# Relative bias, low-rank weights and projection steps rearranged around RWKV in a hybrid RWKV-7 / FoX / DSA layer

## Chip, cores and metric

The kernel runs on one core of a Trainium2 chip, in one launch. The metric is device time in microseconds (us), median of several runs; lower is better.

## The reference

One layer over 1024 prompt rows and 64 sample rows (the latter with 512 cached rows): `u = RMSNorm(h)`, one projection `z = u @ W_in` for all branches, three mixers on slices of `z`, and `h + W_out . concat(gated mixers)`, normed again. The parts that the change touches:

```python
def rwkv7_mixer(z, shift_prev, wkv0, mu, w0, w_b, a0, a_b, ...):
    zm = z + (prev - z) * mu
    r, k, v, w_in, a_in = jnp.split(zm, ...)
    decay = jnp.exp(-jnp.exp(-softplus(-(w0 + jnp.tanh(w_in) @ w_b)) - 0.5))
    a = jax.nn.sigmoid(a0 + a_in @ a_b)
    ...
def dsa_attention(q, k, v, q_idx, k_idx, w_idx, t5_table, q_pos, k_pos):
    ...
    bias = t5_table[t5_bucket(pos_sel - q_pos)]
    s = jnp.where(valid, s + bias, -jnp.inf)
```

A is RWKV-7, whose decay and rate come from two low-rank products (`w_b`, `a_b`, 64 x 512 each); B is FoX, softmax attention with a forget gate; C is DSA, sparse attention over the keys that an indexer picks, with a T5 relative bias.

## The kernel before, in words

The program goes through these stages: load and norm; the indexer of C (`indexer`); RWKV in 17 units of four 64-row chunks each; FoX; DSA and output. The projection runs beside all of them as a fill. A column group of 128 is projected in steps: each step of `proj` is one `yield` and three matmuls (L154), for the high part of `u` and the weights and the two cross terms. `pump(n)` adds `n` to a credit (at most 8) and deals one step for each whole credit, so a stage's rate sets how many steps lie between its own pieces. Rate 70 (capped) holds in the indexer, `R_A` = 7 in the preparation of the first unit (prep0), `R_A / 10` = 0.7 for each piece that `braid` deals in RWKV's units. `tied` writes edges that hold a dealt step behind the piece before it; within these edges a scheduler orders every engine's instructions.

Weights for a column group come through `load_w`: a load into one of two raw buffers (L130, SyncE), a cast to the high part on ScalarE (L137), and the low part and a bf16 copy on POOL (L140, L142). ScalarE also evicts projection banks (L802), with VectorE's L803 behind it.

The relative bias (`relative_bias`, L1242) is a 32x8 table times a one-hot, 8 x 384 (L1254), copied to `t5v`, and written to the DRAM buffer `d_t5`, 128 times the same rows (L1258): one transfer from 8 partitions. DSA reads `d_t5` at the other end of the kernel.

`rwkv_pools` (L1260) loads the low-rank weights twice over (`wabr`, four transfers, L1275), casts them on ScalarE (`wabh`, L1276) and subtracts on POOL (`wabl`, L1278). `low_rank` multiplies with both (L1293, L1294). A unit's inversion (`chunk_invert`) has five levels: a product (L1478) that VectorE masks (Y, L1509), then products with Y (L1471) that VectorE subtracts (U, L1518). The state chain has products at L1559, L1564 and L1572 with VectorE between them.

The lines of the fill's rate, in `pump` and in the loop over the units:

```python
self.credit = min(self.credit + n, 8)
while self.credit >= 1 and self.fill:
    ...
s.weave(("prep0", s.prepare(units[0], x[0])), 10, R_A)
s.braid(work, R_T if u > n else R_END if len(work) < 3 and u else R_A / 10, ...)
```

Of the kernel before, what the change touches and what calls it, by code (L numbers as in the profile page):

```python
# [12 lines left out]
F32 = mybir.dt.float32  # L13
F32R = mybir.dt.float32r
# [4 lines left out]
OP = mybir.AluOpType  # L19
# [5 lines left out]
P = 128  # L25
# [60 lines left out]
class K:  # L86
# [103 lines left out]
    def pump(self, n):  # L190

        self.credit = min(self.credit + n, 8)
        while self.credit >= 1 and self.fill:
            self.mark(self.fill[0][0])
            if self.tied(self.fill[0][1], (PE,)):
                self.credit -= 1
            else:
                self.filled.add(self.fill.popleft()[0])
# [66 lines left out]
        self.now = None  # L265

    now = None


    def setup(self):  # L270
# [127 lines left out]
    def indexer(self):  # L398
# [6 lines left out]
        with ExitStack() as c2:  # L405
            ip, ip2 = self.ip, self.ip2
            pm = self.pool("idx_ps", bufs=3, space=PSUM, ctx=c2)
            KI = ip.tile([P, NKEY], F32R, name="KI")
            KIL = ip.tile([P, NKEY], F32R, name="KIL")
            QI = [ip.tile([P, 832], F32R, name=f"QI{h}") for h in range(4)]  # L410
            mT = ip.tile([P, NT], F32, name="mT")
            mrow = ip.tile([P, 9, 76], F32, name="mrow")
            wI = ip.tile([P, 9, 4], F32, name="wI")
            wm = self.get_w((COL["c_ki"], 68), (COL["b_f"], 8))
            wq = [self.get_w((COL["c_qi"] + 128 * j, 128)) for j in range(2)]

            def both(ps, t0, n):
                c = slice(t0, t0 + n)
                for r in (slice(0, 64), slice(64, 128)):
                    nc.scalar.copy(KI[r, c], ps[0:64, :n])  # L420
                    nc.vector.tensor_tensor(KIL[r, c], ps[0:64, :n], KI[0:64, c], op=OP.subtract)

            def keys(t0, n):
                ps = yield from self.proj(wm, t0, n)
                nc.scalar.copy(mT[:76, t0:t0 + n], ps[:76, :n])
                both(ps, t0, n)

            def queries(j, t0, n):
                ps = yield from self.proj(wq[j], t0, n)
                c0 = t0 - 256  # L430
                a, b = QI[2 * j], QI[2 * j + 1]
                nc.scalar.copy(a[0:64, c0:c0 + n], ps[0:64, :n])
                nc.scalar.copy(b[64:128, c0:c0 + n], ps[64:128, :n])
                nc.vector.tensor_tensor(a[64:128, c0:c0 + n], ps[0:64, :n], a[0:64, c0:c0 + n], op=OP.subtract)
                nc.vector.tensor_tensor(b[0:64, c0:c0 + n], ps[64:128, :n], b[64:128, c0:c0 + n], op=OP.subtract)


            yield from keys(0, 384)
            for j in range(2):
                yield from queries(j, 256, 384)  # L440
            yield from keys(384, 384)

            ps = self.tp()
            for a in range(4):
                nc.tensor.transpose(ps[:64, a * P:(a + 1) * P], self.kc[:, a, :], self.ident)
            both(ps, 1088, 512)
            yield from keys(768, 320)
            for j in range(2):
                yield from queries(j, 640, 448)
            for i in range(9):  # L450
                r = P if i < 8 else 64
                ps = self.tp()
                nc.tensor.transpose(ps[:r, :76], mT[:76, i * P:i * P + r], self.ident[:76, :76])
                nc.scalar.copy(mrow[:r, i, :], ps[:r, :76])
            nc.vector.memset(wI[64:128, 8, :], 0.0)
            nc.vector.tensor_scalar(wI[:, 0:8, :], mrow[:, 0:8, 64:68], 0.5, None, op0=OP.mult)
            nc.vector.tensor_scalar(wI[:64, 8, :], mrow[:64, 8, 64:68], 0.5, None, op0=OP.mult)
            self.fill.extend((f"a{j}", self.park_a(j)) for j in range(2))
            self.pump(8)
            for i in list(range(2, 8)) + ["s"]:  # L460

                if i == 3:
                    gates = self.forget(ip, mrow)
                    next(gates)
                    bias = self.relative_bias(c2)
                    next(bias)
                if i == 4:
                    nc.sync.dma_start(out=O["p_c_kidx"][0, 0].rearrange("(a p) d -> p a d", p=P), in_=mrow[:, 0:8, 0:64])
                    nc.sync.dma_start(out=O["s_c_kidx"][0, 0], in_=mrow[:64, 8, 0:64])
                if i == 5:  # L470
                    next(bias)
                if i == 7:
                    next(gates, None)
                if i == "s":
                    next(bias, None)
                r = P if i != "s" else 64
                q0 = i * P - 256 if i != "s" else 768
                k0, kn = (0, (i + 1) * P) if i != "s" else (1024, 576)
                wi = 8 if i == "s" else i
                for s0 in range(0, kn, 512):  # L480
                    n = min(512, kn - s0)
                    for h in range(4):
                        ps = pm.tile([P, 512], F32, tag="s", name="ps_idx")
                        nc.tensor.matmul(ps[:r, :n], QI[h][:, q0:q0 + r], KI[:, k0 + s0:k0 + s0 + n], start=True, stop=False)
                        nc.tensor.matmul(ps[:r, :n], QI[h][:, q0:q0 + r], KIL[:, k0 + s0:k0 + s0 + n], start=False, stop=True)
                        rl = ip2.tile([P, 512], F32, tag="rl", name="rl")
                        nc.scalar.activation(rl[:r, :n], ps[:r, :n], AF.Relu, scale=0.125)
                        dst = self.score[i][:r, s0:s0 + n]
                        if h == 0:
                            nc.vector.tensor_scalar(dst, rl[:r, :n], wI[:r, wi, 0:1], None, op0=OP.mult)  # L490
                        else:
                            nc.vector.scalar_tensor_tensor(dst, rl[:r, :n], wI[:r, wi, h:h + 1], dst, op0=OP.mult, op1=OP.add)
                        if h % 2:
                            yield
                if i != "s":
                    nc.vector.memset(self.score[i][0:64, kn - 64:kn], NEG)
# [745 lines left out]
    def relative_bias(self, ctx):  # L1242

        nc = self.nc
        self.d_t5 = self.dram.tile([P, 8, 384], F32, tag="d_t5", name="d_t5")
        p = self.pool("t5", ctx=ctx, right=True)
        pp = self.pool("t5p", space=PSUM, ctx=ctx, right=True)
# [7 lines left out]
        vv = p.tile([8, 384], F32, name="t5v")  # L1255
        nc.vector.tensor_copy(vv, ps[:8, :384])
        yield
        nc.sync.dma_start(out=self.d_t5.rearrange("q h r -> h q r"), in_=vv.rearrange("h (o r) -> h o r", o=1).broadcast_to([8, P, 384]))  # L1258


    def rwkv_pools(self, c2):

# [2 lines left out]
        one = self.pool("rw1", ctx=c2, right=True)  # L1265
        self.gen = self.pool("gen", space=PSUM, ctx=c2)
        self.gring = lambda tag, bufs: (lambda dt=F32: self.gen.tile([P, 512], dt, tag=tag, name="ps_" + tag, bufs=bufs))

        self.wabh = one.tile([P, 2, 512], F32R, name="wabh")
        self.wabl = one.tile([P, 2, 512], F32R, name="wabl")  # L1270
        nc.gpsimd.memset(self.wabl.bitcast(F32), 0.0)
        raw = self.z("wabr")[:, 0:1024].rearrange("p (x c) -> p x c", x=2)
        for x, nm in enumerate(("a_w_b", "a_a_b")):
            for r in (slice(0, 64), slice(64, 128)):
                nc.sync.dma_start(out=raw[r, x], in_=I[nm][0])  # L1275
        nc.scalar.copy(self.wabh, raw)  # L1276
        for x, r in enumerate((slice(0, 64), slice(64, 128))):
            nc.gpsimd.tensor_tensor(self.wabl[r, x], raw[r, x], self.wabh[r, x], op=OP.subtract)  # L1278
        self.one, self.state = one, None

        self.ND = [one.tile([P, 2, 4, P], F16, name=f"ND{i}") for i in range(2)]
# [474 lines left out]
def program(ctx, tc, I, O):  # L1756
    s = K(ctx, tc, I, O)
# [23 lines left out]
    s.setup()  # L1781
    cx.close()
    with ExitStack() as c2:
        s.zs = s.pool("zs", bufs=1, ctx=c2, right=True)
        s.scp = s.pool("scp", ctx=c2, right=True)
        s.tkp = s.pool("tkp", ctx=c2, right=True)
# [15 lines left out]
        topk = s.topk()  # L1802
        n = len(units)
        x = [dict(ND=s.ND[u % 2]) for u in range(n)]
        s.weave(("prep0", s.prepare(units[0], x[0])), 10, R_A)
        for u in range(n + 2):
            work = []
# [11 lines left out]
            if u < n:  # L1819
                work.append(("topk", topk, N_TOPK, (DVE, ACT)))  # L1820
            work = [w[:3] for w in work if w[0] != "topk"]
            s.free = u >= FE
            s.braid(work, R_T if u > n else R_END if len(work) < 3 and u else R_A / 10, ("topk", topk, N_TOPK, (DVE, ACT), work[-1][0] if SIDE < 0 else work[SIDE][0]) if u < n else None)
        for _ in topk:
            pass
        s.need("b0")
        for _ in range(PX):
            s.pump(8)
# [85 lines left out]
```

## Time and profile before

| what | value |
|---|---|
| median of 3 runs | 1330.21 us (1328.97 to 1335.14) |
| profiled execution, its own time | 1331.56 us |
| its span | 1329.8 us |
| TensorE (PE) busy | 1258.4 us, 95% |
| VectorE (DVE) busy | 847.5 us, 64% |
| ScalarE (ACT) busy | 780.2 us, 59% |
| GpSimd (POOL) busy | 669.7 us, 50% |
| DMA | 168.78 MB, mean 127 GB/s |
| mean granted TensorE clock | 0.979 |

The busy times are sums over the span of one profiled execution; the engines run beside each other. The span is what lies between the first and the last instruction, and the execution's own time has 1.8 us more around it. The granted clock is the share of TensorE's full speed that the chip let through.

### The profile page before, as it was taken

What the parts mean: (1) busy time and instruction counts of PE and PEld (TensorE: products, weight loads), DVE (VectorE), ACT (ScalarE), POOL (GpSimd) and SP (SyncE); (2) the same over time, 40 slices, a digit from 0 to 9 for tenths busy, and PEclk for the clock granted to TensorE, in tenths of its full rate; (3) what the DMA queues carried; (4) which work ended last, traced back from release to release, by engine and by line L of the source; (5) the groups of instructions that cost most, each with busy time, mean ns of one, the idle gap of its engine ahead of it and who ended that gap; (6) DMA issues with size and microseconds to landing.
All of it is one profiled execution on the core that took longest, in us unless ns stands there. A gap on an engine that the chain in (4) does not pass through costs nothing.

```text
span 1329.8 us, 29357 instructions
## 1 busy us (share of the span) xinstructions
PE 1258.4 (95%) x10544; PEld 964.2 (73%) x10563; DVE 847.5 (64%) x2487; ACT 780.2 (59%) x1762; POOL 669.7 (50%) x973
## 2 busy tenths in 40 slices
PE   7969999999999999988999998999999989999997
PEld 5747676777777777766777677888988856777764
DVE  7338437887877777899754316556666479766642
ACT  7335427777777887644353346576665578655532
POOL 6223445445445456556464365566667567544311
PEclk9979999999999999988999998999999989999999
DMA  7352422222223324433232378867755576543323
GB/s 224 50 105 71 128 83 66 87 70 89 68 70 104 102 80 140 123 101 110 94 104 89 126 216 246 217 201 209 182 198 146 146 212 186 142 116 106 97 76 95
DMA packets 172460, 168.78 MB, mean 127 GB/s; under 512 B 38513, under 2 KB 147097, under 8 KB 172314
## 3 DMA queue, kind: packets, MB, share of 16 engines
q1 hardware_dynamic: 172314, 166.89, 43.9%
q8 instruction: 84, 1.38, 0.4%
q14 instruction: 62, 0.51, 0.1%
HBM read 104.61 MB, written 62.24 MB: 125 GB/s over the span
## 4 chain that ended last, share of the span: by engine, by line
PE 73%; DVE 11%; DMA 6%; ACT 3%; issue 3%; POOL 2%; SPq 1%; DVEq 0%; POOLq 0%; ACTq 0%
PE pproj L154 32%; PE pproj L1697 7%; PE ps_pv L993 5%; PE ps_atp L107 5%; PE ps_tp L1697 4%; PE ps_ga L1412 3%; DMA wraw<-in_w_in_dram 2%; PE ps_sc L962 2%; PE ps_sc L963 2%; PE ps_gb L1471 2%; PE ps_tp L107 1%; PE ps_gb L1478 1%; PE ps_gc L1581 1%; ACT junka L601 1%; PE ps_gc L1583 1%
## 5 line engine op out<-in xcount | busy, mean ns | idle before, releaser
L154 PE MATMUL pproj<-uH,wh 128*128 128x384 f32 (+4 forms) x1088 | 494.6, 455 | 0.0
L154 PE MATMUL pproj<-uH,wl 128*128 128x384 f32 (+4 forms) x1088 | 363.4, 334 | 0.0
L154 PE MATMUL pproj<-uL,wb 128*128 128x384 bf16 (+4 forms) x1088 | 359.4, 330 | 2.2 <-DVE shift L806 2.0
L154 PEld LDWEIGHTS pproj<-uH,wh 128*128 128x128 f32 (+1 forms) x1088 | 217.9, 200 | 3.9 <-issue 0.7
L154 PEld LDWEIGHTS pproj<-uH,wl 128*128 128x128 f32 (+1 forms) x1088 | 208.1, 191 | 2.2 <-issue 0.2
L154 PEld LDWEIGHTS <-wb 128*128 128x128 bf16 (+1 forms) x1088 | 106.6, 98 | 118.6 <-issue 81.5
L601 ACT ACTIVATE junka<-score,tk_tau 128x1024 f16<-128x1024 f32 (+4 forms) x160 | 149.4, 934 | 38.9 <-DVE junk L595 24.1
L914 POOL TENSOR_SCALAR S<-S,mx 128x128 f32<-128x128 f32 (+8 forms) x136 | 103.8, 766 | 83.7 <-DVE mx L913 60.4
L931 ACT CAST hl<-ps_atp 128x512 fp32r<-128x512 f32 (+3 forms) x184 | 93.4, 514 | 77.7 <-PE ps_atp L107 68.2
L140 POOL TENSOR_TENSOR wl<-wraw,wh 128x256 fp32r<-128x256 f32 (+1 forms) x184 | 137.1, 775 | 3.3 <-ACT wh L137 2.7
L932 DVE TENSOR_TENSOR hl<-ps_atp,hl 128x512 fp32r<-128x512 f32 (+3 forms) x184 | 109.7, 600 | 44.6 <-ACT hl L931 42.8
L142 POOL TENSOR_SCALAR wb<-wraw 128x512 bf16<-128x512 f32 (+1 forms) x92 | 60.3, 671 | 142.1 <-issue 60.7
L909 ACT ACTIVATE S<-S,mx 128x128 f32<-128x128 f32 (+8 forms) x136 | 105.8, 778 | 38.2 <-DVE mx L905 34.8
L993 PE MATMUL ps_pv<-hl,VS 128*128 128x256 f32 (+3 forms) x640 | 113.7, 290 | 7.7 <-ACT hl L931 3.2
L993 PEld LDWEIGHTS ps_pv<-hl,VS 128*128 128x128 f32 (+1 forms) x640 | 90.4, 176 | 20.8 <-DVE hl L932 5.0
L107 PE MATMUL ps_atp<-ident,S 128*128 128x128 f32 x616 | 103.6, 280 | 1.1 <-POOL S L914 0.8
L1159 POOL TENSOR_TENSOR cb<-nm,T 128x256 f32<-128x256 bf16 (+2 forms) x80 | 57.4, 724 | 52.7 <-DVE mx L905 51.1
L107 PEld LDWEIGHTS ps_atp<-ident,S 128*128 128x128 f32 x616 | 76.4, 144 | 7.7 <-issue 1.7
L137 ACT CAST wh<-wraw 128x1024 fp32r<-128x1024 f32 (+1 forms) x46 | 47.7, 1038 | 47.0 <-PE pproj L154 27.0
L1697 PE MATMUL pproj<-oh,gh 128*128 128x512 f32 x144 | 67.4, 490 | 0.6 <-ACT pproj L1745 0.3
L803 DVE SCALAR_TENSOR_TENSOR zm<-pproj,omm,zs 128x384 f32<-128x384 f32 (+2 forms) x52 | 25.8, 496 | 43.3 <-ACT zs L802 42.9
L1697 PE MATMUL pproj<-ol,gb 128*128 128x512 bf16 (+1 forms) x134 | 48.8, 386 | 1.4 <-DVE ol L1677 0.9
(383 smaller groups left out, 2849.6 us busy)
## 6 DMA issues: line engine op xcount, KB each, us to landing
wraw<-in_w_in_dram SPq DMA_DIRECT2D x45, 512.0 KB
oraw<-in_w_out_dram SPq DMA_DIRECT2D x12, 512.0 KB
out_dram<-rows SPq DMA_DIRECT2D x10, 512.0 KB
x<-in_x_prompt_dram SPq DMA_DIRECT2D x8, 512.0 KB
wt<-a_wa SPq DMA_DIRECT2D x16, 256.0 KB
b_v<-vs SPq DMA_DIRECT2D x8, 512.0 KB
VS<-b_v SPq DMA_DIRECT2D x8, 512.0 KB
d_y<-y SPq DMA_DIRECT2D x64, 64.0 KB
```

What stands on the lines that cost most here:

```text
L107: self.nc.tensor.transpose(out, x, self.ident[:n, :n])
L140: nc.gpsimd.tensor_tensor(l[:, k:k + 2, :n], raw[:, k:k + 2, :n], h[:, k:k + 2, :n], op=OP.subtract)
L142: nc.gpsimd.tensor_scalar(b[:, k:k + 4, :n], raw[:, k:k + 4, :n], 1.0, 0.0, op0=OP.mult, op1=OP.add)
L154: self.nc.tensor.matmul(ps[:n, :nt], a[:, k, :n], b[:, k, t0:t0 + nt], start=(k == 0 and i == 0), stop=(k == KD - 1 and i == 2))
L601: nc.scalar.activation(junk[:, :sc.shape[1]], sc, AF.Sign, bias=tf[:, j:j + 1], accum_out=cnt[:, j:j + 1])
L909: nc.scalar.activation(S[:, :kn], S[:, :kn], AF.Exp, bias=mx[:, nm - 1:nm], scale=-1.0, accum_out=mx[:, 6:7])
L914: nc.gpsimd.tensor_scalar(S[:, :kn], S[:, :kn], mx[:, 7:8], 0.5, op0=OP.mult, op1=OP.mult)
L931: nc.scalar.copy(ph[:kr, a:b], ps[:kr, a:b])
L932: nc.vector.tensor_tensor(pl[:kr, a:b], ps[:kr, a:b], ph[:kr, a:b], op=OP.subtract)
L993: nc.tensor.matmul(pv[0:m, q0:256], VS[:, kb, 0:m], hl[:, x, o:o + w], start=kb == 0 and x == 0, stop=at[-1][0] == last and n == 3)
L1159: nc.gpsimd.tensor_tensor(o, x, y, op=OP.add)
L1697: nc.tensor.matmul(ps[hf][:n, :], parts[m // 4][q][:, m % 4, :n], self.wo[m][q // 2][:, hf * 512:hf * 512 + 512], start=m == 0 and q == 0, ...
```

## The change

It has three parts. The table's product goes to DRAM as a row of 12 KB (`d_row`) and is copied from there to `d_t5` in eight transfers of 16 rows, which the program text places one at a time at the start of RWKV's units 1 to 8. The low-rank weights are loaded, cast and subtracted in the indexer, in a pool of their own (`lr`), with the raw copy in the score buffer of the indexer's last query block. And `pump` gets a `burst`: with 2, from prep0 to the end of RWKV's loop, it deals only when two steps are due.

```diff
@@ pump
         self.credit = min(self.credit + n, 8)
+        if self.credit < self.burst:
+            return
         while self.credit >= 1 and self.fill:
@@ indexer
-                    bias = self.relative_bias(c2)
-                    next(bias)
+                    self.bias = self.relative_bias(c2)
+                    next(self.bias)
+                    self.load_low_rank()
                 if i == 5:
-                    next(bias)
+                    next(self.bias)
+                    self.split_low_rank()
                 if i == "s":
-                    next(bias, None)
+                    next(self.bias)
@@ relative_bias
+        row = self.dram.tile([8, 384], F32, tag="d_row", name="d_row")
         yield
-        nc.sync.dma_start(out=self.d_t5.rearrange("q h r -> h q r"), in_=vv.rearrange("h (o r) -> h o r", o=1).broadcast_to([8, P, 384]))
+        nc.sync.dma_start(out=row[:, :], in_=vv)
+        yield
+        for q in range(0, P, 16):
+            nc.sync.dma_start(out=self.d_t5[q:q + 16], in_=row.rearrange("(o h) r -> o h r", o=1).broadcast_to([16, 8, 384]))
+            yield
+    def load_low_rank(self):
+        nc, p = self.nc, self.lr
+        self.wabh = p.tile([P, 2, 512], F32R, name="wabh")
+        self.wabl = p.tile([P, 2, 512], F32R, name="wabl")
+        nc.gpsimd.memset(self.wabl.bitcast(F32), 0.0)
+        self.wabr = self.score[7].rearrange("p (x c) -> p x c", x=2)
+        for x, nm in enumerate(("a_w_b", "a_a_b")):
+            for r in (slice(0, 64), slice(64, 128)):
+                nc.sync.dma_start(out=self.wabr[r, x], in_=self.I[nm][0])
+    def split_low_rank(self):
+        nc = self.nc
+        nc.scalar.copy(self.wabh, self.wabr)
+        for x, r in enumerate((slice(0, 64), slice(64, 128))):
+            nc.gpsimd.tensor_tensor(self.wabl[r, x], self.wabr[r, x], self.wabh[r, x], op=OP.subtract)
@@ rwkv_pools
-        self.wabh = one.tile([P, 2, 512], F32R, name="wabh")
-        self.wabl = one.tile([P, 2, 512], F32R, name="wabl")
-        nc.gpsimd.memset(self.wabl.bitcast(F32), 0.0)
-        raw = self.z("wabr")[:, 0:1024].rearrange("p (x c) -> p x c", x=2)
-        for x, nm in enumerate(("a_w_b", "a_a_b")):
-            for r in (slice(0, 64), slice(64, 128)):
-                nc.sync.dma_start(out=raw[r, x], in_=I[nm][0])
-        nc.scalar.copy(self.wabh, raw)
-        for x, r in enumerate((slice(0, 64), slice(64, 128))):
-            nc.gpsimd.tensor_tensor(self.wabl[r, x], raw[r, x], self.wabh[r, x], op=OP.subtract)
@@ program
+        s.lr = s.pool("lr", ctx=c2, right=True)
+        s.burst = 2
         s.weave(("prep0", s.prepare(units[0], x[0])), 10, R_A)
+            if u:
+                next(s.bias, None)
             s.free = u >= FE
+        s.burst = 1
         s.need("b0")
```

What stands on the engines is set by the scheduler. On SyncE, in the indexer, before (t5tab and t5oh are the table and the one-hot, d_t the bias in DRAM, wraw a raw weight buffer, mrow the indexer's keys):

```order
L1250 DMA t5tab<-in_t_table_dram 32x8
L1251 DMA t5oh<-in_onehot_dram 32x384
L1258 DMA d_t_822<-t5v 8x128x384
L130 DMA wraw<-in_w_in_dram 128x8x128 x2
L468 DMA out_dram<-mrow 128x8x64
```

and in the changed kernel, where score_416 is the score buffer that holds the raw low-rank weights:

```order
L1257 DMA t5tab<-in_t_table_dram 32x8
L1258 DMA t5oh<-in_onehot_dram 32x384
L1281 DMA score_416<-in_a_w_b_dram 64x512 x2
L1281 DMA score_416<-in_a_a_b_dram 64x512 x2
L1265 DMA d_row<-t5v 8x384
L1268 DMA d_t_826<-d_row 16x3072 x8
L130 DMA wraw<-in_w_in_dram 128x8x128 x2
L473 DMA out_dram<-mrow 128x8x64
```

All eight copies stand together, ahead of the two weight loads, and not among RWKV's units; the low-rank loads have come up ahead of them.

On POOL, before, where the indexer ends and prep0 begins (ND are two buffers of the inversion, lw the log decay):

```order
L140 TENSOR_TENSOR wl<-wraw,wh 128x256 x4
L1271 MEMSET wabl 128x1024
L1283 MEMSET ND_1695 128x1024
L1283 MEMSET ND_1696 128x1024
L1325 MEMSET lw 128x4
L1278 TENSOR_TENSOR wabl<-wabr,wabh 64x512 x2
L1337 TENSOR_SCALAR lw<-lw 128x4x64
```

and in the changed kernel the same work well before that, in the middle of the indexer:

```order
L140 TENSOR_TENSOR wl<-wraw,wh 128x256 x4
L1277 MEMSET wabl 128x1024
L1287 TENSOR_TENSOR wabl<-score_416,wabh 64x512 x2
L142 TENSOR_SCALAR wb<-wraw 128x512 x2
L140 TENSOR_TENSOR wl<-wraw,wh 128x256 x4
```

The memset and the two subtractions have moved past seven groups of weights, to the gap ahead of the one whose wb follows.

On TensorE, in the first unit's inversion, before (the last product of one kind L1478 of a level, then what lies ahead of the products L1471 that need VectorE's Y):

```order
L1478 LDWEIGHTS ND_1695
L1478 MATMUL ps_gb<-T_2152,ND_1695 128x64
L1363 MATMUL ps_ga<-ident,arn 64x128 x4
L154 LDWEIGHTS wb
L154 MATMUL pproj<-uL,wb 128x384
L154 MATMUL pproj<-uH,wh 128x384
L154 MATMUL pproj<-uH,wl 128x384
L1471 LDWEIGHTS U_2163
L1471 MATMUL ps_gb<-Y_2170,U_2163 64x64
```

and in the changed kernel, where L1495 and L1488 are these lines:

```order
L1495 MATMUL ps_gb<-T_2152,ND_1698 128x64
L1495 LDWEIGHTS ND_1698
L1495 MATMUL ps_gb<-T_2152,ND_1698 128x64
L1488 LDWEIGHTS U_2163
L1488 MATMUL ps_gb<-Y_2173,U_2163 64x64
```

The projection step and the transposes (L1363) between the two have gone elsewhere. Over RWKV, runs of projection matmuls fall from 272 to 238 (runs of one step from 69 to 18).

## Rows read from the trace of the kernel before

**Rows 1.** The page's first part: busy us (share of the span) and instructions of each engine.

```profile
PE 1258.4 (95%) x10544; PEld 964.2 (73%) x10563; DVE 847.5 (64%) x2487; ACT 780.2 (59%) x1762; POOL 669.7 (50%) x973
```

**Rows 2.** The chain of waits from 40 to 175: start us, us, what.

```profile
57.80 26.16 DMA wraw<-in_w_in_dram
...
87.98 4.44 PE pproj L154 x13
...
158.80 4.26 DMA wabr<-in_a_a_b_dram
```

**Rows 3.** TensorE's timeline, 70 to 98: start, us, line, operation, [idle before <- releaser].

```profile
85.65 0.34 PE L453 MATMUL ps_tp<-ident,mT 76*64 76x76 f32 x1 [9.54 <-ACT mrow L454]
87.98 0.50 PE L154 MATMUL pproj<-uL,wb 128*128 128x384 bf16 x1 [2.00 <-DVE shift L806]
```

**Rows 4.** Windows: us, busy PE PEld DVE ACT POOL, granted clock, DMA share, GB/s.

```profile
70.00:75.00 5.00, 5.00 (x34) 3.75 (x33) 0.00 (x0) 0.00 (x0) 0.00 (x0) 1.00 0.44 49
...
175.00:180.00 5.00, 5.00 (x34) 3.37 (x32) 2.95 (x7) 0.58 (x1) 1.23 (x3) 1.00 0.88 270
...
87.98:92.42 4.44, 4.43 (x14) 3.21 (x15) 3.92 (x13) 3.73 (x8) 1.00 (x3) 0.50 0.48 122
165.70:171.30 5.60, 5.59 (x22) 4.49 (x22) 1.29 (x3) 2.74 (x6) 4.03 (x6) 0.50 0.07 21
```

**Rows 5.** TensorE's timeline from 332.8 to 334.3, in RWKV.

```profile
332.99 0.34 PE L154 MATMUL pproj<-uH,wl 128*128 128x384 f32 x1
333.16 0.34 PE L154 MATMUL pproj<-uL,wb 128*128 128x384 bf16 x1
...
333.51 0.34 PE L154 MATMUL pproj<-uH,wl 128*128 128x384 f32 x1
333.78 0.71 PE L1412 MATMUL ps_ga<-QR,BK 64*128 64x128 f32 x4
```

**Rows 6.** SyncE's queue (SPq), 38 to 100: start and length of an issue.

```profile
49.62 0.29 SPq L1258 DMA_DIRECT2D d_t<-t5v  x1
57.80 17.71 SPq L130 DMA_DIRECT2D wraw<-in_w_in_dram  x2
```

**Rows 7.** DMA issues: the write of the relative bias, KB each.

```profile
d_t<-t5v SPq DMA_DIRECT2D x1, 1536.0 KB
```

**Rows 8.** ScalarE's timeline, 66 to 90.

```profile
84.06 1.04 ACT L137 CAST wh<-wraw 128x1024 fp32r<-128x1024 f32 x1 [15.09 <-DMA wraw<-in_w_in_dram]
```

**Rows 9.** TensorE's timeline, 160 to 167, at the start of prep0.

```profile
164.32 0.38 PE L1293 MATMUL ps_ga<-wt,wabh 128*128 128x256 f32 x1 [2.12 <-ACT wabh L1276]
165.71 0.58 PE L1294 MATMUL ps_ga<-wt,wabl 128*128 128x256 f32 x1 [1.01 <-POOL wabl L1278]
```

**Rows 10.** ScalarE's and POOL's timelines, 155 to 170.

```profile
163.22 1.04 ACT L1276 CAST wabh<-wabr 128x1024 fp32r<-128x1024 f32 x1 [2.17 <-DMA wabr<-in_a_a_b_dram]
...
164.40 2.60 POOL L1278 TENSOR_TENSOR wabl<-wabr,wabh 64x512 fp32r<-64x512 f32 x2 [6.05 <-ACT wabh L1276]
```

**Rows 11.** Windows of RWKV: its bulk, and a stretch near its end.

```profile
200.00:560.00 360.00, 349.02 (x4145) 264.37 (x4143) 280.18 (x905) 281.31 (x646) 186.07 (x292) 1.00 0.30 92
...
600.00:625.00 25.00, 21.80 (x210) 15.97 (x210) 23.43 (x57) 12.08 (x33) 16.34 (x20) 0.87 0.26 71
```

**Rows 12.** ScalarE's and POOL's timelines in the indexer.

```profile
47.16 0.42 ACT L425 COPY mT<-pproj 76x320 f32<-76x320 f32 x1 [1.56 <-PE pproj L154]
...
53.64 1.20 POOL L142 TENSOR_SCALAR wb<-wraw 128x512 bf16<-128x512 f32 x2 [21.27 <-PE pproj L154]
```

**Rows 13.** Timeline of all engines, 247.6 to 249.6, in RWKV.

```profile
247.89 0.29 PE L1478 MATMUL ps_gb<-T,ND 128*128 128x64 f16 x4
...
248.22 0.42 DVE L1509 TENSOR_TENSOR Y<-ps_gb,con 128x256 f16<-128x256 f32 x1 [0.28 <-PE ps_gb L1478]
...
248.70 0.31 PE L1471 MATMUL ps_gb<-U,Y 64*64 64x64 f16 x8 [0.25 <-DVE Y L1509]
```

**Rows 14.** A window of the last stage.

```profile
1070.00:1080.00 10.00, 8.50 (x34) 6.81 (x35) 7.27 (x32) 6.74 (x18) 7.88 (x13) 0.67 0.70 215
```

More of the change, by code (lines that the diff above doesn't have):

```diff
@@ L267 @@
     now = None
+    burst = 1
     def setup(self):
```

## Prediction, before the changed kernel had run

> **What bounds the kernel now.** The page's first part comes first: the PE row has TensorE at 95% of the span [rows 1], so the time is nearly all TensorE's work and only its 71 us of idle time and its slow stretches are to be won. The chain of waits then says where TensorE stands still for long early on: two transfers are named in it, a weight load of 26.16 us and a low-rank load of 4.26 us [rows 2]. I read TensorE's timeline at both places.
>
> First stop (A): a transpose starts at 85.65 after 9.54 us of idle time, so TensorE has stood since 76.11, and projection resumes at 87.98 after 2.00 us more [rows 3]. From there 13 projection matmuls take 4.44 us [rows 2] at a granted clock of 0.50, the lower of the two levels [rows 4]; at full clock three of them take some 0.52 us (0.17 from one to the next [rows 5]), so 13 take 2.3 us, and 2.1 us are lost. The reason stands on SyncE and ScalarE. SyncE issues the relative-bias write at 49.62, then two weight loads from 57.80, whose issue takes 17.71 us [rows 6]: the queue is full of the bias write. That write is 1536 KB in one issue [rows 7]. While it runs, the DMA engines are 0.44 busy and move 49 GB/s; where weights flow freely they move 270 GB/s at 0.88 [rows 4]. ScalarE waits 15.09 us for the weights at its cast (L137) [rows 8], and the evictions behind it (L802) that free the projection's banks stand still with it.
>
> Second stop (B): the first low-rank product of RWKV (L1293) waits 2.12 us for the cast of its weights, and the next (L1294) 1.01 us for their low part [rows 9]; cast and subtraction stand at 163.22 and 164.40, right ahead [rows 10]. The stretch behind it is at half clock for 5.60 us [rows 4], of which half is lost, 2.8 us.
>
> Elsewhere TensorE is full: from 200 to 560, the bulk of RWKV, 349.02 of 360 us are busy at clock 1.00 [rows 11].
>
> **The change, part by part.** *Bias copies (A).* By SyncE's order the eight copies do not lie between RWKV's units: all eight stand right behind the 12 KB row, still ahead of the two weight loads. What changes is their shape: from one write out of 8 partitions in runs of 1.5 KB to eight copies of 16 rows of 12 KB. The price of these is in no row. Bounds: at 270 GB/s [rows 4] the 1.57 MB take 5.8 us, at twice the old rate, 98 GB/s (0.44 busy on what looks like half the engines), 16 us, at the old 49 GB/s 32 us. Eight issues at about 0.3 us, as the old one [rows 6], and the row's landing (about 2 us, estimated as half of the 4.26 us that a larger load took [rows 2]) let them start near 52. They end at 58, 68 or 84. The weights leave SyncE at 57.80 at the earliest in any case (their buffer is freed then) and need 2 us at 270 GB/s. ScalarE wants them at 84.06 − 15.09 = 68.97, and TensorE has other work to 76.11; so up to about 74 nothing is lost, which asks for 1.57 MB in 22 us, 71 GB/s. I take the middle rate, since larger pieces on more rows are nearer the weight loads' kind than the old write's. Gain: 9.54 + 2.00 + 2.1 = **−13.6 us**; bounds 0 and −13.6. The nine added issues cost nothing: SyncE idles between 49.62 and 57.80 but for them.
>
> *Low-rank load (B).* Four loads of 128 KB, one cast of 1.05 us, a memset and two subtractions of 1.3 us move from prep0 into the indexer. By the orders the cast now stands before the copy at 47.16, where ScalarE has 1.56 us of idle time, and the subtractions before the POOL row that idled 21.27 us [rows 12]. The cover is that idle time; without it the cast would hold up TensorE's evictions by 1 us. On SyncE the four issues go ahead of the bias row and delay it by nothing: the bias write's issue at 49.62 waits for VectorE's copy of the table, not for SyncE. What is late next at L1293 are the other loads of that unit (keys, rates), issued just ahead of the old ones, and 12 fewer projection matmuls stand in front of it, 2.1 us: I leave 1 us of the 5.9 (2.12 + 1.01 + 2.8) standing and take **−5 us**; bounds 0 and −6.
>
> *Two steps at a time (C).* The number of steps is unchanged, and so is the mean rate; runs of projection matmuls in RWKV fall from 272 to 238 by the order. A switch from projection to a tiled product takes 0.27 us from start to start, where projection matmuls step by 0.17 [rows 5]: 0.10 us per run, and at most as much on the way back, which the row does not show alone. 34 runs fewer give −3.4 to −6.8; I take −4. The TensorE that waits for VectorE between two levels of the inversion is the other side: L1478 at 247.89 makes what VectorE needs, VectorE's row starts at 248.22 and takes 0.42, and L1471 that needs it starts at 248.70, having idled 0.25 with one other product between [rows 13]. From 247.89 + 0.29 to 248.70 is 0.52 us: one step of three matmuls (3 × 0.17) covers it exactly, none leaves it bare, and a second one adds nothing. By TensorE's order the pairs of dependent products (the inversion's, and the state chain's L1559, L1564, L1572) with no projection between rise from 54 to 105 of 406, 51 more. All of TensorE's idle time from 200 to 560, 10.98 us [rows 11], shared among the 54 that are there now makes 0.2 us each; the bare wait is 0.5, and where other products lie between it is 0. I take 0.2: **+10 us**, bounds 0 and +25. C is +6 in sum.
>
> In the Trainium skill, "TensorEngine Tiling (Array Packing)", section Key Properties, it says that changing the tiling mode, not just the tile, drains TensorE. By that rule the count is of mode changes, which fall by 17 only (692 to 675), and the saving would be 1.7 us in place of 4, the total 2 us worse; the row of 0.27 us is such a change and agrees with it.
>
> *The rest (D).* In the last stage the scheduler exchanges some loads and products. The stretch is sensitive, with TensorE busy 8.50 of 10 us at clock 0.67 in one window [rows 14], but nothing in the order prefers a side: 0, bounds ±5. FoX's order is unchanged.
>
> Sum: −13.6 − 5 + 6 + 0 = −12.6. The profiled execution took 1331.56, 1.35 above the median of 1330.21; 1331.56 − 12.6 − 1.35 = **1317.6 us** on the median's scale.
>
> **The rivals.** *1: the uncovered steps cost nothing.* Where no projection stands between, another unit's product often does, and VectorE may be done early. For it: VectorE has a fifth of the stretch free [rows 11]. Against it: the 0.25 us with a product between [rows 13]. C is −4, the time 1330.2 − 13.6 − 5 − 4 = 1307.6.
>
> *2: RWKV becomes bound by its own chain, slower.* At 0.5 us each, 51 steps cost 25.5 us; the 105 bare pairs then idle 52 us of some 400, 3.3 us in 25, what TensorE idles from 600 to 625 (25 − 21.80), where the granted clock is 0.87 [rows 11]. If a fifth of the stage falls to such a clock, 350 × 0.2 × 0.15 adds 10: −18.6 − 4 + 25.5 + 10 = +13, 1343. It decides from 0.57 us per step in all, clock included ((18.6 + 4 + 6.65) / 51). Against it: the mean clock is 1.00 over the bulk of the stage with 54 such pairs. The Trainium skill, "TensorE: Matmul & The Clock Gate", section What's actually happening, says that the throttled state is the default and activity releases it; these rows agree, and by that rule spread-out idle time in RWKV would be paid twice.
>
> *3: the weights still wait (the copies do not get out of the way).* The eight copies stand in the same place as the write did. If they move at the old 49 GB/s, they end near 84 and A is 0: −5 + 6 = +1, 1331. It decides below 71 GB/s. For it: the order. Against it: 16 long rows per copy.
>
> **How the numbers follow.** My forecast has a chance of 0.62, rival 1 0.18, rival 3 0.12, rival 2 0.08. A measurement of this kernel can tell about 0.5%, 6.65 us, from no change: faster is below 1323.6. The forecast's own spread (C from +2 to +15, D ±5) lies from 1309 to 1327, and about 0.04 of it is above 1323.6, with rival 3 that is 0.16 for the same; rival 2 is slower. Faster 0.58 + 0.18 = 0.76. The range goes from 1301 (rival 1 with D at its good end) to 1331 (rival 3); left out are rival 2 and the outer edges.
>
> **What would show it.** A right: TensorE's rows from 70 to 90 without a gap over 1 us, the weight loads' issue under 2 us each, ScalarE's wait at L137 gone, the copies moving over 71 GB/s. A wrong: the cast still starts near 84. B right: the first low-rank product follows projection within 1 us at clock 1.00. C: TensorE's idle time in the 360 us after 200 grows from 11 to some 20; rival 1 if it stays near 11 and the busy sum falls; rival 2 if it reaches 35 and the granted clock of these windows falls below 0.97. The forecast is wrong if A and B both hold and the time is still above 1325, or if the last stage moves by more than 5 us.

## The result, and the profile after

The change made the kernel slower: 1338.14 us (median of 22 runs, 1333.80 to 1346.15) against 1331.32 us (median of 22 runs) of the kernel before; the ratio is 1.0052, with a 95% interval of 1.0039 to 1.0066. The prediction had 1317.6 us and a range that ended at 1331. The profiled execution took 1338.38 us, with a span of 1336.6.

The page's first part has TensorE 6.0 us busier than in [rows 1], in a span 6.8 us longer:

```profile
PE 1264.4 (95%) x10563; PEld 967.1 (72%) x10563; DVE 845.1 (63%) x2487; ACT 778.6 (58%) x1762; POOL 673.2 (50%) x973
```

Both stops that the change was to remove are gone. SyncE's queue, which answers to [rows 6]: eight copies issued in 4.95 us, and the two weight loads behind them in 5.46 us in place of 17.71.

```profile
49.09 0.28 SPq L1265 DMA_DIRECT2D d_row<-t5v  x1
50.50 4.95 SPq L1268 DMA_DIRECT2D d_t<-d_row  x8
57.25 5.46 SPq L130 DMA_DIRECT2D wraw<-in_w_in_dram  x2
```

The windows over the copies, and two of those that hold the old stop (granted clock, DMA share and GB/s stand last): the copies move at 270 to 289 GB/s, where the old write moved 49 [rows 4], and TensorE is busy throughout at clock 1.00.

```profile
52.00:54.00 2.00, 2.00 (x14) 1.44 (x12) 0.00 (x0) 0.74 (x1) 0.82 (x2) 1.00 0.92 270
54.00:56.00 2.00, 2.00 (x12) 1.36 (x12) 0.68 (x2) 1.49 (x4) 1.99 (x4) 1.00 1.01 289
...
75.00:80.00 5.00, 5.00 (x30) 3.73 (x28) 4.49 (x17) 4.47 (x9) 1.56 (x3) 1.00 0.42 112
80.00:85.00 5.00, 5.00 (x31) 3.73 (x30) 4.93 (x12) 2.84 (x5) 2.36 (x3) 1.00 0.73 173
```

The cast whose wait was 15.09 us [rows 8] starts at 71.34 and waits for nothing that loads (ScalarE's timeline), and the low-rank products follow projection with no wait, where [rows 9] had 2.12 and 1.01 us (TensorE's timeline):

```profile
71.34 1.05 ACT L137 CAST wh<-wraw 128x1024 fp32r<-128x1024 f32 x1 [2.89 <-PE pproj L154]
```

```profile
146.03 0.34 PE L154 MATMUL pproj<-uH,wl 128*128 128x384 f32 x1
146.20 0.28 PE L1310 MATMUL ps_ga<-wt,wabh 128*128 128x256 f32 x1
146.32 0.28 PE L1311 MATMUL ps_ga<-wt,wabl 128*128 128x256 f32 x1
```

The first of these started at 164.32 before, at 146.20 now: RWKV begins 18.1 us earlier. Its end gives it all back. From the first low-rank product to the first score product of FoX (L962, now L968) the windows are, of the kernel before and of the change:

```profile
164.30:791.80 627.50, 602.88 (x6607) 452.73 (x6607) 427.91 (x1311) 385.06 (x893) 328.88 (x501) 0.98 0.33 100
```

```profile
146.20:796.90 650.70, 609.71 (x6620) 457.42 (x6619) 425.18 (x1312) 386.70 (x894) 332.70 (x499) 0.98 0.32 97
```

RWKV takes 23.2 us longer; TensorE idles 41.0 us in it in place of 24.6. Behind RWKV 1.7 us are added. −18.1 + 23.2 + 1.7 is the 6.8 us of the span.

### The profile page after: what moved, and what is told of

Same layout as the page of the kernel before. It is cut to its first block, busy times and chain, and to the rows that moved or that the text cites. A ratio compares the mean times of both kernels' runs of the same rounds, so it can differ in the third digit from the quotient of the medians.

```text
span 1336.6 us, 29381 instructions
## 1 busy us (share of the span) xinstructions
PE 1264.4 (95%) x10563; PEld 967.1 (72%) x10563; DVE 845.1 (63%) x2487; ACT 778.6 (58%) x1762; POOL 673.2 (50%) x973
## 4 chain that ended last, share of the span: by engine, by line
PE 74%; DVE 11%; DMA 5%; ACT 4%; issue 3%; POOL 1%; SPq 1%; DVEq 0%; POOLq 0%; ACTq 0%
PE pproj L154 35%; PE pproj L1714 6%; PE ps_pv L999 4%; PE ps_atp L107 4%; PE ps_tp L1714 4%; PE ps_ga L1429 2%; PE ps_sc L968 2%; PE ps_sc L969 2%; PE ps_gb L1488 2%; PE ps_tp L107 1%; PE ps_gc L1598 1%; ACT junka L607 1%; PE ps_gb L1495 1%; PE ps_gc L1589 1%; PE ps_gc L1600 1%
## 5 line engine op out<-in xcount | busy, mean ns | idle before, releaser
L607 ACT ACTIVATE junka<-score,tk_tau 128x1024 f16<-128x1024 f32 (+4 forms) x160 | 149.3, 933 | 40.7 <-DVE tk_tau L621 18.1
L1165 POOL TENSOR_TENSOR cb<-nm,T 128x256 f32<-128x256 bf16 (+2 forms) x80 | 52.7, 665 | 67.5 <-DVE mx L911 58.6
L1714 PE MATMUL pproj<-ol,gb 128*128 128x512 bf16 (+1 forms) x144 | 52.8, 387 | 1.4 <-DVE ol L1694 1.4
L1434 POOL TENSOR_SCALAR ND<-BN 64x256 f16<-64x256 f32 x34 | 13.7, 403 | 78.3 <-DVE BN L1433 78.1
```

The costliest lines, as they stand in the source:

```text
L607: nc.scalar.activation(junk[:, :sc.shape[1]], sc, AF.Sign, bias=tf[:, j:j + 1], accum_out=cnt[:, j:j + 1])
L1165: nc.gpsimd.tensor_tensor(o, x, y, op=OP.add)
L1714: nc.tensor.matmul(ps[hf][:n, :], parts[m // 4][q][:, m % 4, :n], self.wo[m][q // 2][:, hf * 512:hf * 512 + 512], start=m == 0 and q == 0, ...
```

## The experiments

In the table, RWKV's start and length are read as above from TensorE's timeline of each profile; idle is TensorE's in that stretch; "behind" is from there to the end of the span; bare are the pairs of dependent products with no projection between, by TensorE's order. Ratios are to the kernel before on the same chip, with 95% intervals.

| run | time, us | ratio | start | RWKV | idle | behind | bare |
|---|---|---|---|---|---|---|---|
| before | 1331.32 | 1 | 164.3 | 627.5 | 24.6 | 538.0 | 54 |
| change | 1338.14 | 1.0052 (1.0039 to 1.0066) | 146.2 | 650.7 | 41.0 | 539.7 | 105 |
| no bursts | 1318.02 | 0.9904 (0.9873 to 0.9935) | 147.4 | 632.9 | 24.1 | 540.0 | 37 |
| bursts alone | 1356.15 | 1.0195 (1.0160 to 1.0229) | 165.3 | 648.0 | 38.8 | 544.7 | 102 |
| four at a time | 1361.81 | 1.0241 (1.0212 to 1.0270) | 147.5 | 675.7 | 49.3 | 540.0 | 162 |
| one matmul at a time | 1325.28 | 0.9949 (0.9921 to 0.9977) | 147.9 | 629.7 | 17.2 | 541.0 | 11 |
| bias copies alone | 1316.71 | 0.9894 (0.9864 to 0.9924) | 150.6 | 629.1 | 23.5 | 534.8 | 54 |
| low-rank load alone | 1330.12 | 0.9996 (0.9974 to 1.0017) | 161.3 | 627.6 | 22.9 | 539.0 | 37 |
| single behind the inversion | 1310.42 | 0.9840 (0.9814 to 0.9867) | 146.3 | 620.5 | 23.1 | 539.4 | 34 |
| two behind inversion and chain alone | 1334.41 | 1.0017 (0.9998 to 1.0037) | 147.1 | 649.8 | 34.4 | 536.0 | 135 |
| one copy of 128 rows | 1319.45 | one run | 146.6 | 630.6 | 26.1 | 540.6 | 37 |
| direct in eight pieces | 1330.88 | one run | 162.5 | 628.9 | 22.7 | 537.7 | 37 |
| bias copies, single behind the inversion | 1316.03 | 0.9880 (0.9861 to 0.9900) | 151.1 | 621.4 | 21.8 | 541.5 | 34 |
| three, single behind the inversion | 1310.54 | 0.9846 (0.9819 to 0.9873) | 146.0 | 620.4 | 23.4 | 540.9 | 19 |

**Is it the deals by twos?** First the change without them:

```diff
-        s.burst = 2
+        s.burst = 1
```

> The change with steps dealt one at a time again (burst 1); the bias copies and the early low-rank load stay. Pairs of dependent RWKV products with no projection between: 37 by TensorE's order, against 105 in the change and 54 before. Theory (bare pairs cost RWKV what A and B had won): the lead of some 20 us at RWKV's start stays to the end, the loss of 26 us in RWKV goes, 1308 to 1315 us. Rival 1 (RWKV loses the lead whatever the deals are, since it starts earlier and is bound by VectorE's or ScalarE's search for the top keys): 1328 to 1338. Rival 2 (the late stage eats it): lead intact to 700 us, time above 1322.

Measured 1318.02 us. The lead at RWKV's start stays, 16.9 us, and of the 23.2 us that RWKV had lost 17.8 are back. Rivals 1 and 2 fall. The time is 3 us above what was expected: RWKV is still 5.4 us longer than before. Of these, 3.0 us are matmul time at full clock (some 2 us of it are 12 projection matmuls that before stood ahead of RWKV's first product) and 2.9 us are slow clock; the idle time is 0.5 us shorter. The profiled execution took 1322.04 us, 4.0 above the median, so some of the 5.4 us belongs to this execution alone. The last section comes back to one place in it.

Then the kernel before with `burst = 2` and nothing else:

> The kernel before with two steps at a time and nothing else; 102 bare pairs against 54. Theory: A and B's stops stay as before and RWKV takes some 25 us longer, 1350 to 1360 us. Rival 1 (bursts are harmless): 1325 to 1333.

Measured 1356.15 us, RWKV 20.5 us longer: the deals alone do it, with no lead to lose. Another 6.7 us are added behind RWKV, and why was not looked into. Then the dose, four steps in place of two, on the change:

```diff
-        s.burst = 2
+        s.burst = 4
```

> The change with four steps at a time; 162 bare pairs against 105, 173 runs of projection against 238. Theory: 57 more at some 0.5 us, 28 us, 1360 to 1370 us, with TensorE's idle time in RWKV up by 15 to 20 us and its granted clock down. Rival (it is the number of switches that counts): 65 runs fewer at 0.1 to 0.2 us, faster than the change by 6 to 13 us, 1325 to 1332.

Measured 1361.81 us, 23.7 us above the change. With 65 runs of projection fewer it is dearer, so fewer switches are not what counts. But the theory hit the time by other terms than its own: idle time rose by 8.3 us, not by 15 to 20, and of the 25.0 us that RWKV is longer than in the change 14.7 are slow clock. A window of this run in RWKV:

```profile
347.00:372.00 25.00, 19.16 (x189) 14.13 (x188) 16.37 (x55) 16.31 (x36) 11.36 (x18) 0.80 0.26 77
```

TensorE stands for 5.84 of 25 us, and the granted clock is 0.80. And the other way, one matmul at a time:

```diff
+                if self.part < 1 and i < 2:
+                    yield
...
-        while self.credit >= 1 and self.fill:
+        while self.credit >= self.part - 1e-6 and self.fill:
-                self.credit -= 1
+                self.credit -= self.part
...
-        s.burst = 2
+        s.part = 1 / 3
```

> The change with projection dealt one matmul at a time (a third of a step) from prep0 to RWKV's end, at the same mean rate; 11 bare pairs, 346 runs of projection. Theory: 26 bare pairs fewer than with one step (13 us at most, since single matmuls cover 0.17 us and not 0.52), and 58 more switches at 0.1 to 0.2 us, 6 to 12 us dearer: 1305 to 1315 us, near the run with one step. Rival (a thin cover is as bad as none): 1320 to 1335.

The time lies in the rival's range, but not for the rival's reason: TensorE's idle time in RWKV is the lowest of all, 17.2 us. RWKV is no shorter than before, since the matmul time at full clock rises, from 596.2 us in the run with no bursts (288 runs of projection) to 610.0 (346 runs). The runs spread over 1316 to 1331 us, the median is at 1325.28; why they spread more than others stays open.

**What are the two other parts worth?** Each alone, on the kernel before:

> The kernel before with the relative bias through the DRAM row and eight copies, and nothing else: low-rank load where it was, steps one at a time. Theory: the stop at 76 to 88 us and the slow clock behind it go, 13.6 us, and TensorE's order in RWKV stays that of the kernel before (54 bare pairs): 1315 to 1319 us. Rival (the stop moves to the next weight load): 1325 to 1331.

> The kernel before with the low-rank weights loaded in the indexer, and nothing else; 37 bare pairs against 54. Theory: 5 us less at the start of RWKV, 1322 to 1327 us, with the stop of 9.5 us at the weight load still there. Rival (the run with both parts and no bursts lost 5 us of its lead in RWKV since the low-rank load shifts TensorE's order against VectorE's): 1327 to 1333, the gain at the start given back.

The copies alone: 1316.71 us, RWKV starts 13.7 us earlier and is 1.6 us longer. The low-rank load alone starts RWKV 3.0 us earlier, and the time can't be told from that of the kernel before. Here the rival's range was right; where the gain goes is taken up under B below.

**What makes the copy fast?** The detour through the DRAM row is there with one transfer in place of eight (`self.d_t5[:, :, :]` from the row broadcast to 128), or the eight pieces of 16 queries without the row (straight from `t5v`), both on the run with no bursts.

> The run with no bursts, with the eight copies from the DRAM row put into one transfer of 128 rows. Theory (the long runs out of DRAM are what makes the copy fast, not its being cut): the copy moves at 250 GB/s or more as in the change, the weight loads go out at 57 us in under 3 us each, no stop at 76 us, 1313 to 1320 us. Rival (one large transfer blocks the queue whatever it is made of): the stop of 9 us stays, 1326 to 1333.

> The run with no bursts, with the write of the bias cut into eight pieces of 16 queries but still straight from the 8 partitions of SBUF in runs of 1.5 KB. Theory: the same 49 to 53 GB/s as the one write of before, the weights land at 83 to 86 us, the stop of 9 us stays, 1326 to 1333 us. Rival (the cutting was what helped): no stop, 1313 to 1320.

SyncE's queue with one copy, and two windows of that run:

```profile
50.88 0.54 SPq L1267 DMA_DIRECT2D d_t<-d_row  x1
57.62 5.45 SPq L130 DMA_DIRECT2D wraw<-in_w_in_dram  x2
```

```profile
52.00:54.00 2.00, 2.00 (x12) 1.49 (x12) 0.00 (x0) 0.36 (x1) 0.45 (x1) 1.00 0.78 276
54.00:56.00 2.00, 2.00 (x12) 1.29 (x10) 0.31 (x1) 1.87 (x4) 1.98 (x4) 1.00 0.84 313
```

The same with the direct pieces, SyncE's queue and a window, and where TensorE starts again in its timeline:

```profile
50.37 23.49 SPq L1265 DMA_DIRECT2D d_t<-t5v  x8
73.97 7.94 SPq L130 DMA_DIRECT2D wraw<-in_w_in_dram  x2
```

```profile
70.00:75.00 5.00, 5.00 (x34) 3.82 (x32) 0.27 (x1) 0.00 (x0) 0.00 (x0) 1.00 0.45 53
```

```profile
87.35 0.34 PE L457 MATMUL ps_tp<-ident,mT 76*64 76x76 f32 x1 [10.49 <-ACT mrow L458]
```

It is the row in DRAM that counts, not the parts. One copy of 1.5 MB moves at 276 to 313 GB/s; eight pieces out of the 8 partitions move at 53, hold the queue for 23.49 us, and TensorE stops for 10.49 us. The row changes two things at once, the source (DRAM in place of 8 partitions) and the length of a run (12 KB in place of 1.5 KB); which of them counts was not separated.

**Which cover is it?** Two at a time stay, except behind one kind of piece:

```diff
-        if self.credit < self.burst:
+        if self.credit < (1 if self.now in ("invert",) else self.burst):
```

> The change with two steps at a time behind every piece of RWKV except the inversion's, where they are dealt one at a time: 34 bare pairs (105 in the change), 272 runs of projection. Theory (a bare pair is what costs): near the run with no bursts, 1313 to 1322 us. Rival (bursts cost by themselves, through evictions that come in twos): 1330 to 1340, as the change.

Measured 1310.42 us, faster than the kernel before by 1.6% and the fastest of all. Of the change's 41.0 us of idle time 23.1 are left, about what the kernel before has (24.6), so bursts elsewhere cost nothing that can be seen; RWKV's window shows a clock of 1.00:

```profile
146.30:766.80 620.50, 597.37 (x6620) 448.32 (x6619) 423.14 (x1312) 386.21 (x894) 329.08 (x499) 1.00 0.33 102
```

That it is also faster than the run with no bursts has another reason. Idle time (23.1 and 24.1 us) and matmul time at full clock (596.0 and 596.2) are the same; of the 12.4 us between the two profiles in RWKV 11.1 are slow clock, 1.4 us against 12.5. In the four profiles that share the order of the run with no bursts this loss lies between 6.9 and 12.5 us, so a part of the difference is the execution's luck; what took the rest away was not settled.

The reverse keeps two at a time behind the pieces of `invert` and `chain`, and one elsewhere:

> The reverse: two at a time behind the inversion's and the state chain's pieces, one at a time elsewhere: 135 bare pairs, 227 runs. Theory: 30 bare pairs more than the change at 0.3 to 0.45 us, 1346 to 1354 us. Rival (bursts themselves): half of the change's loss, 1325 to 1332.

Measured 1334.41 us, between the two ranges. RWKV is 649.8 us long, as in the change (650.7), so two at a time behind these pieces alone are enough for the whole loss. But it is not larger, though 135 pairs are bare in place of 105; TensorE idles 34.4 us, less than 41.0, and that RWKV is as long even so lies in slow clock (14.9 us against 12.0) and matmul time at full clock (600.5 against 597.7). The number of bare pairs puts runs in a rough order and is no price. Part of what else sets it can be read from the traces: the inversion's products wait for VectorE as often as in the change (21 times against 20), but of their 9.1 us VectorE spends only 1.2 on other instructions that stand ahead, in the change 7.4 of 15.8.

Last, two tries for a better version: the copies without the early low-rank load, and three at a time except behind the inversion.

> The bias in copies, the low-rank load where it was before, two steps at a time except behind the inversion's pieces; 34 bare pairs, 270 runs. Theory (the early low-rank load is worth nothing to 3 us): 1310 to 1314 us. Rival (in that order of TensorE it is the low-rank load that let it gain): 1316 or more.

> The change with three steps at a time except behind the inversion's pieces, where they come one at a time: 19 bare pairs, 277 runs. Theory (what is kept covered costs nothing): 1306 to 1313 us, with TensorE idle in RWKV below 25 us. Rival (bunching by itself costs, in evictions and buffers): above 1318.

The first missed its range at 1316.03, where its rival had put it: RWKV starts 4.8 us later than with the low-rank load and is as short, and 2.1 us are lost behind it. So where TensorE's RWKV is well covered the early load seems to keep its gain; the intervals of the two ratios (0.9861 to 0.9900, and 0.9814 to 0.9867) just overlap, so this is likely and not shown. Three at a time, 1310.54 us, is as good as two.

## Why the prediction was wrong

**What bounds the kernel, A, the copies.** Right in mechanism and size: −13.6 us was forecast, and the copies alone start RWKV 13.7 us earlier. The middle rate, 98 GB/s, was too careful; 270 and more came of it. It made no difference, since by the prediction's own margin 71 GB/s were enough. Rival 3 fell with it.

**B, the low-rank load.** −5 us was forecast. The start of RWKV's first product, 3.0 us earlier alone, can't show it: of the terms only the wait of 2.12 us lies ahead of that product, 1.01 and the 2.8 of the slow stretch lie behind it, and 12 projection matmuls (some 2 us) have moved behind it as well. A later place in the work shows it better. With the load alone the 800th projection matmul comes 5.2 us earlier than in the kernel before, and 19.0 us in the run with no bursts, where A and B together were to give 18.6; in the first 9 us of RWKV the granted clock is 1.00 in place of 0.62. So the size was right there. Its cover held: the cast stood at 45.11 in ScalarE's idle time and the next eviction started at 46.63. What the step missed is that the gain does not last by itself: the load shifts the order of RWKV, the lead is lost again further on in it (the last section shows one place), and alone it came to nothing measurable.

**C, two at a time: the step that failed.** The forecast was +10 for idle time and −4 for switches, within bounds from −7 to +25; RWKV measured +23.2. Summed over windows of 4 us, the busy time times one less the granted clock is 9.7 us before and 12.0 in the change; so of the 23.2 us 16.4 are idle time, 2.3 clock, and 4.5 matmul time at full clock. Against the forecast of +6 the idle time is 6.4 over, the saving for switches is 4 short, and the other 6.8 are two terms that the sum had at nothing.

The idle time was sized wrongly, by sharing the 10.98 us of [rows 11] among 54 pairs, 0.2 us each; 16.4 us on 51 pairs are 0.32. The two counts do not belong together: the 10.98 us are those of 360 us, the 54 pairs and the 51 more are those of all RWKV, 627.5 us, in which TensorE idled 24.6. In the 360 us alone the forecast came true, idle time of 19.5 us where some 20 were named as the sign (the same window, in the change, which is some 18 us ahead at its start):

```profile
200.00:560.00 360.00, 340.53 (x3970) 256.21 (x3970) 270.24 (x876) 269.66 (x616) 181.57 (x278) 0.99 0.29 88
```

The rest of RWKV, which the share left out, went from 13.6 us to 21.5. What the share could not show either is how long a wait is once nothing covers it. [Rows 13] had VectorE start at once, and 0.52 us stood as the worst. In the change TensorE's timeline and then VectorE's show this:

```profile
438.19 0.29 PE L1495 MATMUL ps_gb<-T,ND 128*128 128x64 f16 x4
...
440.68 0.31 PE L1488 MATMUL ps_gb<-Y,U 64*64 64x64 f16 x8 [1.93 <-DVE Y L1526]
```

```profile
437.94 0.62 DVE L1386 TENSOR_TENSOR BK<-QR,tha 128x256 f32<-128x256 f32 x1
438.59 0.83 DVE L1387 TENSOR_TENSOR BK<-BK,Pi 128x256 f32<-128x256 f32 x1
439.35 0.94 DVE L1390 TENSOR_TENSOR QR<-QR,Pt 128x256 f32<-128x256 f32 x1
440.21 0.41 DVE L1526 TENSOR_TENSOR Y<-ps_gb,con 128x256 f16<-128x256 f32 x1
```

The product is done by 438.5, but in VectorE's row three instructions of the next unit's preparation stand ahead of Y. It starts 1.7 us late, and TensorE waits 1.93 us. VectorE is as busy over RWKV as before (425.18 us against 427.91), but before a projection step more often stood in such places. In the whole stage the waits of the inversion's products on the Y of its levels rise from 1.7 us in 3 (longest 1.2) to 7.1 in 8 (rows of the waits, of before and of the change):

```profile
PE ps_gb L1471 <- DVE Y L1509: 1.7, 3, 1.2
```

```profile
PE ps_gb L1488 <- DVE Y L1526: 7.1, 8, 1.9
```

With the waits on the last Y, on U and on T, all that the inversion's products wait for goes from 4.3 us to 17.2, and what the state chain's products wait for from 5.6 to 9.3. Together that is 16.6 us more, so the added idle time stands in the inversion and the state chain, where the prediction had looked for it.

How much of it is queue can be read too. Of the 15.8 us that the inversion's products wait for VectorE in the change, VectorE spends 6.8 on the instruction that is waited for and 7.4 on others ahead of it; before, it was 1.9 and 0.9 of 3.3 us. So the bare wait is not the latency of one instruction on an idle VectorE alone, but about as much again for its queue, and this was in reach of the profile: VectorE is busy 280 of 360 us in [rows 11], and the prediction used that only to say that a fifth is free.

The saving for switches never came. The matmul time at full clock (length less idle time less clock) is 593.2 us before, 597.7 in the change with 34 runs fewer, 599.7 with 99 fewer; some 2 us are the 12 projection matmuls that were no longer ahead of RWKV. The extra 0.10 us in [rows 5] is there, but with fewer runs it did not add up to a term. Only the other way a price shows: one matmul at a time, with 58 runs more than with no bursts, took 13.8 us more. Of the Trainium skill's rule ("TensorEngine Tiling (Array Packing)", Key Properties) these runs show only that 17 mode changes fewer were worth nothing that can be seen.

**D, the rest.** 0 ± 5 was forecast; 1.7 us were added behind RWKV, in the change, and from −3 to +7 in the experiments.

**The rivals.** The time came out where the prediction said that it would be wrong: A and B hold, and it is above 1325 us. Rival 2 was nearest, RWKV slower with TensorE bare between its dependent products, but its signs did not come: the 360 us have 19.5 us of idle time and not 35, and a granted clock of 0.99 and not below 0.97. It priced idle time at 25.5 and clock at 10 us, and had both too high; 23.2 us over 51 pairs are 0.45 us, below the 0.57 us from which it was to be slower by half a per cent, and with D the result is just at that mark; that it came out slower at all is in part the missing saving of 4 us. A chance of 0.08 was too little: all that spoke against it was a stage that ran well with half as many bare pairs.

## What to carry to other kernels

Work that fills gaps between dependent products is worth where it stands, not how much of it there is: the same steps, dealt in twos everywhere, cost 20 us, and dealt in twos except behind the inversion's products, which another engine must answer, cost nothing; they even gained 8 us over single steps, most of it in the granted clock and for a reason not settled. A wait that a fill covers is to be sized by the queue of the engine that answers, not only by that engine's one instruction, and a price per pair by idle time and pairs of the same stretch. And a broadcast out of a few partitions is cheap to mend: through a row in DRAM it ran over five times as fast.

## What the runs showed of the hardware

One VectorE instruction stood still while GpSimd ran several, and the rows suggest that it stood behind them. In the run with no bursts a 128 x 8 operation that takes 0.17 us at the median took 3.59 us (VectorE's timeline, then POOL's, then windows):

```profile
280.38 3.59 DVE L621 TENSOR_TENSOR tk_tau<-tk_tau,tk_t 128x8 int32<-128x8 int32 x1
284.00 0.42 DVE L1433 TENSOR_TENSOR BN<-ps_ga,con 128x256 f32<-128x256 f32 x1
```

```profile
280.01 1.19 POOL L142 TENSOR_SCALAR wb<-wraw 128x512 bf16<-128x512 f32 x2
281.18 2.77 POOL L140 TENSOR_TENSOR wl<-wraw,wh 128x256 fp32r<-128x256 f32 x4
```

```profile
281.00:284.00 3.00, 1.44 (x14) 0.90 (x11) 2.97 (x1) 0.27 (x1) 2.95 (x5) 1.00 0.00 0
284.00:287.00 3.00, 2.09 (x24) 1.47 (x24) 3.00 (x11) 2.72 (x6) 1.07 (x2) 0.94 0.01 3
287.00:290.00 3.00, 3.00 (x26) 2.46 (x25) 1.65 (x10) 0.87 (x4) 0.00 (x0) 0.50 0.80 251
290.00:293.00 3.00, 3.00 (x15) 1.95 (x15) 1.05 (x3) 2.94 (x8) 1.39 (x2) 0.50 0.39 115
```

It ended when POOL's six instructions in a row ended, at 283.95. TensorE idled 2.5 us for it and then ran at half clock for some 6 us. The run with the low-rank load alone, whose TensorE and VectorE have the same order, has it at the same instruction:

```profile
294.20 3.59 DVE L621 TENSOR_TENSOR tk_tau<-tk_tau,tk_t 128x8 int32<-128x8 int32 x1
```

So do the other two runs with that order, one copy and direct pieces, each 3.59 us. In the kernel before and in the copies alone, where the order is another, that operation takes 1.8 us at most, at another place; in the change 0.6, and in the fastest run 0.7. It is where the run with no bursts lost the most: its 961st projection matmul comes 20.8 us earlier than that of the kernel before, its 1057th, some 37 us on, 15.2. The run with the low-rank load alone goes from 7.0 to 2.9 there. The Trainium skill, "SBUF — State Buffer", section SBUF: two separate sides, says that VectorE with two inputs in SBUF and GpSimd reading SBUF exclude each other for a whole instruction; the operation has two such inputs, and the rows agree, but the hold lasted to the end of POOL's unbroken row, not of one instruction. That moving POOL's work away would end it was not tried.
